# A masked-sum and product kernel: column sums at the tail, and first transfers of 32 and 96 rows in place of 128

## Chip, cores, metric

One Trainium2 chip, one core. The time is that of the device in microseconds (us). Kernels that are compared ran in turn on the same chip, unless it is said otherwise. A run more than 1.5% above the fastest of the same kernel is called slow.

## The reference

```
B, S, D = 8, 8192, 512                    # x: [8, 8192, 512] f32, w: [512, 512] f32
cs  = np.cumsum(x * mask, axis=1)         # mask: position < lengths[b]
mid = cs[b, lengths[b] // 2, :]
out = mid @ w                             # [8, 512]
```

So row b of the output is the sum of the first n = min(lengths // 2 + 1, lengths) rows of x[b], times w. For the lengths drawn here n is 570, 2690, 256, 2057, 905, 3772, 3859 and 571: in whole blocks of 512 rows 1, 5, 0, 4, 1, 7, 7 and 1, and a remainder each.

## The kernel before

A block of 512 rows is loaded as [128 partitions, 4 rows of 512]: 8 KB for each partition, 1 MB in all. TensorE adds it with four matmuls of 8 weight columns in four column groups (eight instructions in the profile, `x8`), so `s_ps` holds four partial sums. SP issues the blocks; ACT issues the remainders. The sequences go in pairs, q = 0 and 1, each side with its own buffers.

```
NP = 6                                              # block buffers for each side
nc.scalar.dma_start(out=wt[:], in_=w.rearrange("(p kc) d -> p kc d", kc=KC)).then_inc(s_w, 16)
nc.sync.dma_start(out=first[:], in_=xf[:BLK].rearrange("(p g) d -> p g d", g=G)).then_inc(s_first, 16)
# (cut) TensorE, for each sequence of each pair
take(pe, s_rem[q], 16 * (len(PARTS) + 1))           # the remainder first
for j in range(G):
    mm = add(j, cur[:, q, B + j * B:2 * B + j * B], rem[:, q, j])
def add_block(k):
    for _ in range(2 if k else 0):                  # fillers, meant to keep the clock up
        pe.matmul(idle_ps[:], lhsT=idle[:, :P], rhs=idle[:], start=True, stop=True)
    take(pe, s_full[q][k], 16)
    for j in range(G):
        mm = add(j, cur[:, q, :B], xt[:, q, k, j])
    mm.then_inc(s_sum, 1)                           # SP waits on it before it refills a buffer
# (cut) tail: DVE copies s_ps to s_sb; four matmuls s_sb^T @ fold; DVE copy; sixteen matmuls with wt; copy; output
```

## Time and profile before

| | before |
|---|---|
| time, first three runs | 88.41, 89.12, 88.33 us |
| profiled run | 89.17 us, span 87.4 us |
| moved | 31.29 MB, mean 358 GB/s over the span |
| second but last block landed | 76.70 us |
| issue of the output | 84.59 us |

The span is what the profile covers; the time is some 1.8 us longer. The lines of the page are in the prediction. From slice 2 to slice 34 the transfers move 356 to 432 GB/s, in most slices 410 or more, so the middle is bound by bytes, and only the start and the tail can change. A transfer has landed when its semaphore has its full count.

### The profile page before, as it was taken

How to read it: one execution, taken by the hardware profiler on the slowest of the kernel's cores; microseconds unless marked ns; L12 is line 12 of the kernel's file. 1: busy time of each engine (PE TensorE's matmuls, PEld its weight loads, DVE VectorE, ACT ScalarE, POOL GpSimd, SP SyncE). 2: the span in 40 equal slices, each digit the busy share in tenths (PEclk: the TensorE clock that was granted, in tenths of full speed). 3: DMA queues.
4: the chain of work that ended last, by engine and by line, in shares of the span. 5: the costliest groups of instructions: out<-in, count | busy, mean ns of one | idle time of the engine just before them, and what ended most of it. 6: DMA issues, size and time to landing. Idle time of an engine off the chain costs nothing. (4 is left out here: it accounts for less than half of the span.)

```text
span 87.4 us, 1387 instructions
## 1 busy us (share of the span) xinstructions
PE 57.3 (66%) x350; PEld 11.0 (13%) x350; DVE 10.6 (12%) x42; ACT 2.0 (2%) x4; POOL 4.4 (5%) x9
## 2 busy tenths in 40 slices
PE   0920355699999798418675569966955556489740
PEld 0220000121111211000210010101110110021520
DVE  3977600000000100000000000000000000000430
ACT  0000000000000000000006000000000000000020
POOL 5940000000000000000000000000000000000000
PEclk9999999999999999999999955599999999965999
DMA  2799999999999999999999999999999999960000
GB/s 30 311 424 356 384 384 408 432 420 424 413 398 416 420 424 428 418 399 417 420 424 428 412 425 424 424 420 420 420 420 424 424 424 420 420 259 0 0 0 11
DMA packets 4694, 31.29 MB, mean 358 GB/s; under 512 B 658, under 2 KB 674, under 8 KB 946
## 3 DMA queue, kind: packets, MB, share of 16 engines
q1 hardware_dynamic: 3762, 27.27, 75.8%
q10 hardware_dynamic: 928, 3.97, 11.7%
q14 instruction: 3, 0.02, 0.1%
q8 instruction: 1, 0.02, 0.1%
HBM read 31.23 MB, written 0.02 MB: 358 GB/s over the span
## 5 line engine op out<-in xcount | busy, mean ns | idle before, releaser
L381 PE MATMUL s_ps<-xt,cur 128*8 128x512 f32 x200 | 31.1, 680 | 12.1 <-PEq L108 12.1
L381 PE MATMUL s_ps<-rem,cur 128*8 128x512 f32 x64 | 11.7, 763 | 6.5 <-PEq L108 6.5
L415 PE MATMUL idle_ps<-idle 128*128 128x512 bf16 x34 | 11.7, 429 | 0.0
L381 PEld LDWEIGHTS s_ps<-xt,cur 128*8 128x8 f32 x200 | 4.3, 90 | 28.2 <-issue 27.9
L355 DVE COPY cur<-table 128x40 f32<-128x40 f32 x8 | 1.4, 184 | 50.4 <-PE s_ps L381 50.4
L381 PE MATMUL s_ps<-first,first_w 128*8 128x512 f32 x8 | 1.9, 1040 | 4.0 <-DVE table L301 4.0
L415 PEld LDWEIGHTS idle_ps<-idle 128*128 128x128 bf16 x34 | 2.0, 100 | 17.8 <-issue 17.8
L381 PEld LDWEIGHTS s_ps<-rem,cur 128*8 128x8 f32 x64 | 1.8, 91 | 15.6 <-issue 15.5
L389 PE MATMUL s_ps<-zero 1*128 1x512 f32 x2 | 2.1, 1132 | 2.3 <-DVE ones L301 2.3
L289 POOL MEMSET rem<- 128x4096 f32 x1 | 3.5, 3512 | 0.0
L301 DVE COPY s_sb<-s_ps 128x256 f32<-128x256 f32 x2 | 0.8, 424 | 19.4 <-PE s_ps L381 19.4
L301 DVE TENSOR_SCALAR n_i<-lens 1x8 int32<-1x8 int32 x1 | 2.8, 2767 | 0.2 <-DMA lens<-in_lengths_dram 0.2
L275 ACT ACT_TABLE_LOAD x1 | 1.3, 1283 | 46.4 <-issue 46.4
L431 PE MATMUL mf_ps<-fold,s_sb 128*128 128x8 f32 x8 | 1.1, 260 | 0.5 <-DVE s_sb L301 0.5
L392 PE MATMUL n_ps<-n_f,ones 1*128 1x8 f32 x2 | 0.6, 368 | 1.2 <-DVE n_f L301 1.2
L278 ACT COPY o_sb<-o_ps 8x128 f32<-8x128 f32 x2 | 0.5, 259 | 36.0 <-PE o_ps L439 36.0
L431 PEld LDWEIGHTS mf_ps<-fold,s_sb 128*128 128x128 f32 x8 | 1.0, 190 | 1.8 <-DVE s_sb L301 1.8
L439 PE MATMUL o_ps<-wt,mf_sb 128*8 128x128 f32 x32 | 1.1, 273 | 0.0
L392 PEld LDWEIGHTS n_ps<-n_f,ones 1*128 1x128 f32 x2 | 0.5, 308 | 2.8 <-DVE n_f L301 2.8
L389 PEld LDWEIGHTS s_ps<-zero 1*128 1x128 f32 x2 | 0.5, 304 | 2.3 <-DVE ones L301 2.3
L439 PEld LDWEIGHTS o_ps<-wt,mf_sb 128*8 128x8 f32 x32 | 0.8, 89 | 0.0
L301 DVE COPY o_sb<-o_ps 8x128 f32<-8x128 f32 x2 | 0.6, 280 | 0.9 <-PE o_ps L439 0.8
(37 smaller groups left out, 6.7 us busy)
## 6 DMA issues: line engine op xcount, KB each, us to landing
xt<-in_x_dram SPq DMA_DIRECT2D x25, 1024.0 KB, 14.3
rem<-in_x_dram ACTq DMA_DIRECT2D x3, 512.0 KB, 7.6
wt<-in_w_dram ACTq DMA_DIRECT2D x1, 1024.0 KB, 6.6
first<-in_x_dram SPq DMA_DIRECT2D x1, 1024.0 KB, 8.4
rem<-in_x_dram ACTq DMA_DIRECT2D x3, 256.0 KB, 6.8
rem<-in_x_dram ACTq DMA_DIRECT2D x3, 128.0 KB, 7.1
rem<-in_x_dram ACTq DMA_DIRECT2D x3, 32.0 KB, 5.7
rem<-in_x_dram ACTq DMA_DIRECT2D x1, 64.0 KB, 6.2
```

What stands on the lines that cost most here:

```text
L275: act.copy(out=warm[:], in_=zero[:, :1])
L278: copy = act.copy(out=o_sb[1][:, j * P:(j + 1) * P], in_=o_ps[64 + 32 * j:64 + 32 * j + B, :P])
L289: pool.memset(rem[:], 0.0).then_inc(s_pool, 1)
L301: do(*args, **kw).then_inc(s_dve, 1)
L355: dve.tensor_copy(out=cur[:, b % 2], in_=table[:, b * WT:(b + 1) * WT]).then_inc(s_cur[b % 2], 1)
L381: return pe.matmul(s_ps[32 * j:32 * j + B], lhsT=weights, rhs=rows, start=False, stop=False, skip_group_check=True, tile_position=(0, 32 * j))
L389: pe.matmul(s_ps[:], lhsT=zero[:, :P], rhs=zero[:], start=True, stop=False, skip_group_check=True)
L392: pe.matmul(n_ps[:, :B], lhsT=ones[:], rhs=n_f[:], start=True, stop=True).then_inc(s_pe, 1)
L415: pe.matmul(idle_ps[:], lhsT=idle[:, :P], rhs=idle[:], start=True, stop=True)
L431: mm = pe.matmul(mf_ps[h][:, i * B:(i + 1) * B], lhsT=s_sb[:, 2 * h + i], rhs=fold[:], start=True, stop=True)
L439: mm = pe.matmul(o_ps[32 * j:32 * j + B, :P], lhsT=mf_sb[:, kc], rhs=wt[:, kc, j * P:(j + 1) * P], start=(kc == 0), stop=(kc == KC - 1), t ...
```

## The change

Intent: (1) bring the first bytes in sooner, with a short first transfer on each queue, 32 rows, two for each of the 16 DMA engines; (2) take the last block out of the sum over rows, so that after it only 16 small matmuls, a transpose and the product follow; (3) keep TensorE's clock up with more fillers (in the profile before, half clock followed stretches in which PE was busy 41% and 43%). Buffers go from six to five a side, and the last block gets a place of its own.

```diff
-    NP = 6
+    NP = 5
-    nc.scalar.dma_start(out=wt[:], in_=w.rearrange("(p kc) d -> p kc d", kc=KC)).then_inc(s_w, 16)
-    nc.sync.dma_start(
-        out=first[:], in_=xf[:BLK].rearrange("(p g) d -> p g d", g=G)
-    ).then_inc(s_first, 16)
+    for at, count in [(0, 32), (32, P - 32)]:
+        part = slice(at, at + count)
+        nc.scalar.dma_start(
+            out=wt[part], in_=w[KC * at:KC * (at + count)].rearrange("(p kc) d -> p kc d", kc=KC)
+        ).then_inc(s_w, 16)
+        nc.sync.dma_start(
+            out=xt[part, 0, 0], in_=xf[G * at:G * (at + count)].rearrange("(p g) d -> p g d", g=G)
+        ).then_inc(s_full[0][0] if at else s_first, 16)
 (cut: SP leaves out the last whole block of the last sequence and loads it at the end, in two halves of
  each partition's rows, to `last`; counts come from a small table; POOL's memset is halved)
+                        keep_busy()                      # two fillers ahead of every remainder
                         take(pe, s_cur[q], 1)
                         take(pe, s_rem[q], 16 * (len(PARTS) + 1))
 (cut)
+                keep_busy()
+                for j in range(4):                       # column sums of all but the last block
+                    if j % 2 == 0:
+                        pe.wait_ge(s_dve, DVE_MASK + 1 + j // 2)
+                    mm = add_column(j, fold[:], s_sb, start=True)
+                with pe.If_cmp(ns[B], 1, "IS_GE"):
+                    keep_busy()
+                    for g in range(G):                   # the last block, 16 matmuls of 128 columns
+                        if g % 2 == 0:
+                            pe.wait_ge(s_last[g // 2], 16)
+                        for j in range(4):
+                            mm = add_column(j, cur[:, 1, :B], last[:, g], start=False)
 (cut: two transposes of 128x64 on DVE in place of the second copy, then the product as before)
```

More of the change, by code (lines that the diff above doesn't have):

```diff
@@ L64 @@
     xt = sb("xt", [P, 2, NP, G, D])
-    first = sb("first", [P, G, D])
+    last = sb("last", [P, G, D])
     rem = sb("rem", [P, 2, G, D])
@@ L68 @@
     lens1 = sb("lens1", [1, 2 * B], I32)
-    warm = sb("warm", [1, 1])
     n_i = sb("n_i", [1, B], I32)
     n_f = sb("n_f", [1, B])
+    cut = sb("cut", [1, 1])
+    blk_i = sb("blk_i", [1, B + 1], I32)
     ones = sb("ones", [1, P])
-    zb = sb("zb", [1, 32], BF16)
     cnt = sb("cnt", [P, B], I32)
@@ L81 @@
     thr = sb("thr", [P, G], I32)
-    first_w = sb("first_w", [P, B])
     idle = sb("idle", [P, D], BF16)
@@ L85 @@
     cur = sb("cur", [P, 2, WT])
-    zero = sb("zero", [1, D])
+    zero = sb("zero", [1, P])
     fold_i = sb("fold_i", [P, B], I32)
     fold = sb("fold", [P, B])
-    s_sb = sb("s_sb", [P, KC, P])
-    mf_sb = sb("mf_sb", [P, KC, B])
+    s_sb = sb("s_sb", [P, D])
+    t_sb = sb("t_sb", [P, KC, 32])
     o_sb = [sb(f"o_sb{h}", [B, D // 2]) for h in range(2)]
     s_ps = ps("s_ps", [P, D])
-    mf_ps = [ps(f"mf_ps{h}", [P, D]) for h in range(2)]
+    t_ps = ps("t_ps", [P, D])
     o_ps = ps("o_ps", [P, D])
@@ L101 @@
     s_cur = [sem(f"cur{q}") for q in range(2)]
-    s_w, s_first, s_len1, s_go, s_out = sem("w"), sem("first"), sem("len1"), sem("go"), sem("out")
+    s_last = [sem(f"last{h}") for h in range(2)]
+    s_zero = [sem(f"zero{q}") for q in range(2)]
+    s_w, s_first = sem("w"), sem("first")
+    s_len1, s_go, s_out = sem("len1"), sem("go"), sem("out")
     s_pool, s_dve, s_pe = sem("pool"), sem("dve"), sem("pe")
@@ L108, in take, with __init__, rows @@
         eng.wait_ge(s, n).then_inc(s, -n)
-    class Counts:
-        def __init__(self, eng, ready, count, loaded=B):
+    class Pairs:
+        def __init__(self, eng, ready, count):
             self.eng = eng
-            self.raw = [eng.alloc_register(f"n_{eng.engine.name}_{i}") for i in range(2 * loaded)]
-            self.regs = self.raw[::2]
+            self.raw = [eng.alloc_register(f"n_{eng.engine.name}_{i}") for i in range(4)]
             self.t = eng.alloc_register(f"t_{eng.engine.name}")
+            self.at = eng.alloc_register(f"pair_{eng.engine.name}")
+            eng.reg_mov(self.at, 0)
             eng.wait_ge(ready, count)
-            eng.load(self.raw, lens1[:, :2 * loaded])
-            self.pair = None
-            if loaded < B:
-                self.pair = eng.alloc_register(f"pair_{eng.engine.name}")
-                eng.reg_mov(self.pair, 0)
-        def without_first(self, base=None):
-            alu, t, n = self.eng.reg_alu, self.t, self.rows(0)
-            alu(t, n, 9, ALU.logical_shift_right)
-            alu(t, t, 1, ALU.min)
-            alu(t, t, 9, ALU.logical_shift_left)
-            alu(n, n, t, ALU.subtract)
-            if base is not None:
-                alu(base, base, t, ALU.add)
-            alu(n, n, 1, ALU.logical_shift_left)
-            alu(n, n, 1, ALU.subtract)
-            alu(n, n, 0, ALU.max)
-        def rows(self, b):
-            n = self.regs[b]
+            eng.load(self.raw, lens1[:, :4])
+        def rows(self, q):
+            n = self.raw[2 * q]
             self.eng.reg_alu(self.t, n, 1, ALU.logical_shift_right)
@@ L147, in rows, with step @@
             return n
-        def next_pair(self):
-            if self.pair is not None:
-                self.eng.reg_alu(self.pair, self.pair, 4, ALU.add)
-                self.eng.reg_alu(self.pair, self.pair, 2 * B - 4, ALU.min)
-                self.eng.load(self.raw, lens1[:, ds(self.eng.snap(self.pair, min_val=0, max_val=2 * B - 4), 4)])
-                return
-            for to, of in zip(self.regs, self.regs[2:]):
-                self.eng.reg_mov(to, of)
+        def step(self):
+            alu, top = self.eng.reg_alu, 2 * B - 4
+            alu(self.at, self.at, 4, ALU.add)
+            alu(self.at, self.at, top, ALU.min)
+            self.eng.load(self.raw, lens1[:, ds(self.eng.snap(self.at, min_val=0, max_val=top), 4)])
     def whole_blocks(eng, n, most, body, k=0):
@@ L163, in whole_blocks @@
                 whole_blocks(eng, n, most, body, k + 1)
-    DVE_SEL, DVE_N, DVE_MASK = 2, 6, 28
+    DVE_SEL, DVE_N, DVE_BLK, DVE_MASK = 1, 5, 10, 31
     DVE_LAST = DVE_MASK + 6
     nc.sync.dma_start(out=lens1[:], in_=lens_words).then_inc(s_len1, 16)
-    nc.scalar.dma_start(out=wt[:], in_=w.rearrange("(p kc) d -> p kc d", kc=KC)).then_inc(s_w, 16)
-    nc.sync.dma_start(
-        out=first[:], in_=xf[:BLK].rearrange("(p g) d -> p g d", g=G)
-    ).then_inc(s_first, 16)
+    for at, count in [(0, 32), (32, P - 32)]:
[6 more added lines that the diff above has]
+        ).then_inc(s_full[0][0] if at else s_first, 16)
     block = nc.Block(no_gpsimd_drain=True)
@@ L183, in _ @@
     def _(sp):
-        ns = Counts(sp, s_len1, 16, loaded=2)
-        sp.sem_inc(s_go, 1)
+        alu = sp.reg_alu
         base, at = sp.alloc_register("sp_base"), sp.alloc_register("sp_at")
         sp.reg_mov(base, 0)
-        ns.without_first(base)
         items = sp.alloc_register("sp_items")
-        sp.reg_mov(items, 2)
+        sp.reg_mov(items, 1)
         until = [[sp.alloc_register(f"until{q}_{k}") for k in range(NP)] for q in range(2)]
@@ L194, in _ @@
             sp.reg_mov(u, 1)
+        has_last, last_at = sp.alloc_register("has_last"), sp.alloc_register("last_at")
+        sp.reg_mov(has_last, 0)
+        sp.reg_mov(last_at, 0)
+        least = sp.alloc_register("sp_least")
+        sp.reg_mov(least, BLK)
+        ns = Pairs(sp, s_len1, 16)
+        sp.sem_inc(s_go, 1)
         with sp.Fori(0, B // 2):
@@ L197, in _, with load @@
                 n = ns.rows(q)
-                sp.reg_alu(items, items, 1, ALU.add)
-                def load_block(k):
-                    sp.wait_ge(s_sum, until[q][k % NP])
-                    sp.reg_alu(items, items, 1, ALU.add)
-                    sp.reg_mov(until[q][k % NP], items)
+                alu(items, items, 1, ALU.add)
+                if q == 0:
+                    alu(n, n, least, ALU.max)
+                    sp.reg_mov(least, 0)
+                else:
+                    with sp.If_cmp(ns.at, 2 * B - 4, "IS_GE"):
+                        alu(has_last, n, 9, ALU.logical_shift_right)
+                        alu(has_last, has_last, 1, ALU.min)
+                        alu(last_at, has_last, 9, ALU.logical_shift_left)
+                        alu(n, n, last_at, ALU.subtract)
+                        alu(last_at, n, ~(BLK - 1), ALU.bitwise_and)
+                        alu(last_at, last_at, base, ALU.add)
+                def load(k):
                     sp.dma_start(
@@ L207, in load_block @@
                     ).then_inc(s_full[q][k % NP], 16)
-                whole_blocks(sp, n, NB, load_block)
-                sp.reg_alu(base, base, S, ALU.add)
-                sp.reg_alu(base, base, ~(S - 1), ALU.bitwise_and)
-            ns.next_pair()
+                def load_block(k):
+                    sp.wait_ge(s_sum, until[q][k % NP])
+                    alu(items, items, 1, ALU.add)
+                    sp.reg_mov(until[q][k % NP], items)
+                    if (q, k) == (0, 0):
+                        with sp.If_cmp(ns.at, 1, "IS_GE"):
+                            load(k)
+                    else:
+                        load(k)
+                whole_blocks(sp, n, NB, load_block)
+                alu(base, base, S, ALU.add)
+            ns.step()
+        with sp.If_cmp(has_last, 1, "IS_GE"):
+            from_rows = rows(sp, at, last_at, 0, BLK).rearrange("(p g) d -> p g d", g=G)
+            for h in range(2):
+                sp.dma_start(
+                    out=last[:, 2 * h:2 * h + 2], in_=from_rows[:, 2 * h:2 * h + 2]
+                ).then_inc(s_last[h], 16)
         sp.wait_ge(s_dve, DVE_LAST)
@@ L219, in _ @@
     def _(act):
-        ns = Counts(act, s_go, 1)
-        t = ns.t
+        alu = act.reg_alu
         base, at = act.alloc_register("act_base"), act.alloc_register("act_at")
         act.reg_mov(base, 0)
-        ns.without_first(base)
         items = act.alloc_register("act_items")
-        act.reg_mov(items, 2)
+        act.reg_mov(items, 1)
         until = [act.alloc_register(f"until_rem{q}") for q in range(2)]
@@ L229, in _ @@
             act.reg_mov(u, 1)
-        act.wait_ge(s_pool, 2)
+        least = act.alloc_register("act_least")
+        act.reg_mov(least, 1)
+        act.memzero(rem[:, 0]).then_inc(s_zero[0], 1)
+        ns = Pairs(act, s_go, 1)
+        t = ns.t
         with act.Fori(0, B // 2):
@@ L233, in _ @@
                 n = ns.rows(q)
+                act.wait_ge(s_zero[q], 1)
                 act.wait_ge(s_sum, until[q])
-                act.reg_alu(items, items, 1, ALU.add)
-                act.reg_alu(until[q], items, 1, ALU.max)
-                act.reg_alu(t, n, 9, ALU.logical_shift_right)
-                act.reg_alu(items, items, t, ALU.add)
+                alu(items, items, 1, ALU.add)
+                alu(until[q], items, 1, ALU.max)
+                alu(t, n, 9, ALU.logical_shift_right)
+                if q == 0:
+                    alu(t, t, least, ALU.max)
+                    act.reg_mov(least, 0)
+                alu(items, items, t, ALU.add)
                 for count, start, step, g in PARTS:
-                    act.reg_alu(t, n, count, ALU.bitwise_and)
+                    alu(t, n, count, ALU.bitwise_and)
                     with act.If_cmp(t, 1, "IS_GE"):
-                        act.reg_alu(t, n, ~(2 * count - 1), ALU.bitwise_and)
+                        alu(t, n, ~(2 * count - 1), ALU.bitwise_and)
                         act.dma_start(
@@ L248, in _ @@
                         act.sem_inc(s_rem[q], 16)
-                act.reg_alu(at, n, ~63, ALU.bitwise_and)
-                act.reg_alu(at, at, base, ALU.add)
-                act.reg_alu(t, n, 63, ALU.bitwise_and)
+                alu(at, n, ~63, ALU.bitwise_and)
+                alu(at, at, base, ALU.add)
+                alu(t, n, 63, ALU.bitwise_and)
                 def load_last(count):
-                    last = rem[3::4, q, 2:] if count > 32 else rem[3:4 * count:4, q, 2:3]
+                    to = rem[3::4, q, 2:] if count > 32 else rem[3:4 * count:4, q, 2:3]
                     act.dma_start(
-                        out=last,
-                        in_=xf[ds(act.snap(at), count)].rearrange("(g p) d -> p g d", g=last.shape[1]),
+                        out=to,
+                        in_=xf[ds(act.snap(at), count)].rearrange("(g p) d -> p g d", g=to.shape[1]),
                     ).then_inc(s_rem[q], 16)
@@ L269, in _ @@
                             act.sem_inc(s_rem[q], 16)
-                act.reg_alu(base, base, S, ALU.add)
-                act.reg_alu(base, base, ~(S - 1), ALU.bitwise_and)
-            ns.next_pair()
-        act.wait_ge(s_dve, DVE_SEL)
-        act.copy(out=warm[:], in_=zero[:, :1])
+                alu(base, base, S, ALU.add)
+            ns.step()
         act.wait_ge(s_pe, B + 5)
@@ L288, in _ @@
         pool.iota(fold_i[:], pattern=[[-1, B]], base=128, channel_multiplier=1).then_inc(s_pool, 1)
-        pool.memset(rem[:], 0.0).then_inc(s_pool, 1)
         pool.memset(idle[:], 1.0).then_inc(s_pool, 1)
+        pool.wait_ge(s_dve, DVE_BLK)
+        pool.memset(rem[:, 1], 0.0).then_inc(s_zero[1], 1)
     @block.vector
@@ L304, in _ @@
         step(dve.memset, zero[:], 0.0)
-        step(dve.memset, zb[:], 0.0)
         assert done == DVE_SEL
@@ L312, in _ @@
         step(dve.tensor_tensor, out=n_f[:], in0=n_i[:], in1=lens1[:, ::2], op=ALU.min)
-        assert done == DVE_N
+        assert done == DVE_N, done
+        step(dve.tensor_copy, out=blk_i[:, :B], in_=n_f[:])
+        step(dve.tensor_scalar, out=blk_i[:, :1], in0=n_f[:, :1], scalar1=BLK, scalar2=None, op0=ALU.max)
+        step(dve.tensor_scalar, out=cut[:], in0=n_f[:, B - 1:], scalar1=BLK, scalar2=None, op0=ALU.is_ge)
+        step(dve.tensor_copy, out=blk_i[:, B:], in_=cut[:])
+        step(dve.scalar_tensor_tensor, out=blk_i[:, B - 1:B], in0=cut[:], scalar=float(-BLK),
+             in1=n_f[:, B - 1:], op0=ALU.mult, op1=ALU.add)
+        assert done == DVE_BLK, done
         step(dve.memset, table[:], 0.0)
@@ L316, in _ @@
         step(dve.memset, tab[:, :, 0:1], 1.0)
-        step(dve.memset, o_ps[:, :P], 0.0)
-        step(dve.memset, first_w[:], 0.0)
+        step(dve.memset, t_ps[:, :P], 0.0)
         step(dve.memset, bits[:], 256)
@@ L342, in _ @@
         step(dve.tensor_copy, out=cnt[:], in_=n_ps[:, :B])
-        step(dve.tensor_scalar, out=first_w[:, :1], in0=cnt[:, :1], scalar1=BLK, scalar2=None,
+        step(dve.tensor_scalar, out=table[:, :1], in0=cnt[:, :1], scalar1=BLK, scalar2=None,
              op0=ALU.is_ge)
@@ L355, in _ @@
             dve.tensor_copy(out=cur[:, b % 2], in_=table[:, b * WT:(b + 1) * WT]).then_inc(s_cur[b % 2], 1)
-        ns = Counts(dve, s_go, 1)
+        n = [dve.alloc_register(f"n_dve_{b}") for b in range(B)]
+        dve.load(n, blk_i[:, :B])
         total, due = dve.alloc_register("total"), dve.alloc_register("due")
-        dve.reg_mov(total, B + 2)
-        ns.without_first()
-        for b in range(B):
-            n = ns.rows(b)
-            dve.reg_alu(n, n, 9, ALU.logical_shift_right)
-            dve.reg_alu(total, total, n, ALU.add)
-        dve.reg_alu(due, total, B + 2, ALU.max)
+        dve.reg_mov(total, B + 1)
+        for r in n:
+            dve.reg_alu(r, r, 9, ALU.logical_shift_right)
+            dve.reg_alu(total, total, r, ALU.add)
+        dve.reg_alu(due, total, B + 1, ALU.max)
         dve.wait_ge(s_sum, due)
-        cols = s_ps[:].rearrange("p (i kc) -> p kc i", kc=KC)
         for h in range(2):
-            step(dve.tensor_copy, out=s_sb[:, 2 * h:2 * h + 2], in_=cols[:, 2 * h:2 * h + 2])
+            step(dve.tensor_copy, out=s_sb[:, 2 * P * h:2 * P * (h + 1)], in_=s_ps[:, 2 * P * h:2 * P * (h + 1)])
+        dve.wait_ge(s_pe, B + 3)
         for h in range(2):
-            dve.wait_ge(s_pe, B + 2 + h)
-            step(dve.tensor_copy, out=mf_sb[:, 2 * h:2 * h + 2].rearrange("p a b -> p (a b)"), in_=mf_ps[h][:, :2 * B])
+            step(dve.transpose, out=t_sb[:, 2 * h:2 * h + 2].rearrange("p k c -> p (k c)"),
+                 in_=t_ps[:, :P].rearrange("p (c k) -> p k c", k=KC)[:, 2 * h:2 * h + 2])
         assert done == DVE_LAST - 2
@@ L383, in add, with keep_busy, add_column @@
                              tile_position=(0, 32 * j))
+        def keep_busy():
+            for _ in range(2):
+                pe.matmul(idle_ps[:], lhsT=idle[:, :P], rhs=idle[:], start=True, stop=True)
+        def add_column(j, weights, row, **kw):
+            return pe.matmul(t_ps[32 * j:32 * j + B, :P], lhsT=weights, rhs=row[:, P * j:P * (j + 1)],
+                             stop=False, skip_group_check=True, tile_position=(0, 32 * j), **kw)
         with pe.Fori(0, 2) as i:
@@ L388, in _ @@
                 pe.wait_ge(s_dve, DVE_SEL)
-                pe.matmul(s_ps[:], lhsT=zero[:, :P], rhs=zero[:], start=True, stop=False,
-                          skip_group_check=True)
+                pe.matmul(s_ps[:], lhsT=zero[:], rhs=zero[:, :1].to_broadcast((1, D)), start=True,
+                          stop=False, skip_group_check=True)
                 pe.wait_ge(s_dve, DVE_N)
                 pe.matmul(n_ps[:, :B], lhsT=ones[:], rhs=n_f[:], start=True, stop=True).then_inc(s_pe, 1)
-                pe.wait_ge(s_pool, 3)
-                ns = Counts(pe, s_go, 1)
-                ns.without_first()
+                pe.wait_ge(s_pool, 2)
+                pe.wait_ge(s_dve, DVE_BLK)
+                ns = [pe.alloc_register(f"n_pe_{b}") for b in range(B + 1)]
+                pe.load(ns, blk_i[:])
                 pe.wait_ge(s_dve, DVE_MASK)
                 pe.wait_ge(s_first, 16)
-                for j in range(G):
-                    mm = add(j, first_w[:], first[:, j])
-                mm.then_inc(s_sum, 1)
                 with pe.Fori(0, B // 2):
                     for q in range(2):
+                        keep_busy()
                         take(pe, s_cur[q], 1)
@@ L409, in _ @@
                         mm.then_inc(s_sum, 1)
-                        n = ns.rows(q)
+                        n = ns[q]
                         def add_block(k):
-                            for _ in range(2 if k else 0):
-                                pe.matmul(idle_ps[:], lhsT=idle[:, :P], rhs=idle[:], start=True,
-                                          stop=True)
+                            if k:
+                                keep_busy()
                             take(pe, s_full[q][k], 16)
@@ L425, in _ @@
                             pe.reg_alu(n, n, 0, ALU.max)
-                    ns.next_pair()
-                for h in range(2):
-                    pe.wait_ge(s_dve, DVE_MASK + 1 + h)
-                    for i in range(2):
-                        mm = pe.matmul(mf_ps[h][:, i * B:(i + 1) * B], lhsT=s_sb[:, 2 * h + i],
-                                       rhs=fold[:], start=True, stop=True)
+                    for to, of in zip(ns[:B], ns[2:B]):
+                        pe.reg_mov(to, of)
+                keep_busy()
[3 more added lines that the diff above has]
+                    mm = add_column(j, fold[:], s_sb, start=True)
+                mm.then_inc(s_pe, 1)
+                with pe.If_cmp(ns[B], 1, "IS_GE"):
+                    keep_busy()
+                    for g in range(G):
[3 more added lines that the diff above has]
+                            mm = add_column(j, cur[:, 1, :B], last[:, g], start=False)
                     mm.then_inc(s_pe, 1)
-                pe.wait_ge(s_w, 16)
+                with pe.Else():
+                    pe.sem_inc(s_pe, 1)
+                pe.wait_ge(s_w, 32)
                 for kc in range(KC):
@@ L438, in _ @@
                     for j in range(4):
-                        mm = pe.matmul(o_ps[32 * j:32 * j + B, :P], lhsT=mf_sb[:, kc],
+                        mm = pe.matmul(o_ps[32 * j:32 * j + B, :P], lhsT=t_sb[:, kc, :B],
                                        rhs=wt[:, kc, j * P:(j + 1) * P],
```

## The prediction

> **What bounds the kernel now.** I read the page first (busy shares, the 40 slices, the chain), then the timeline of the last 13 us, then the arrivals of the DMAs, then quarter-microsecond windows of the start. The slices say that the transfer engines set the middle:
>
> ```profile
> span 87.4 us, 1387 instructions
> PEclk9999999999999999999999955599999999965999
> DMA  2799999999999999999999999999999999960000
> GB/s 30 311 424 356 384 384 408 432 420 424 413 398 416 420 424 428 418 399 417 420 424 428 412 425 424 424 420 420 420 420 424 424 424 420 420 259 0 0 0 11
> ```
>
> One slice is 2.18 us. From slice 2 to 34 DMA is at 90% or more and some 424 GB/s; all 31.29 MB must pass. So the middle cannot shrink: neither kernel changes the rows read. What can change is the ramp at the left and everything after the last byte at the right. The chain of waits agrees, it covers only the tail:
>
> ```profile
> 76.84 4.50 PE s_ps L381 x24
> 81.36 0.44 DVE s_sb L301
> 81.84 1.07 PE mf_ps L431 x8
> 82.91 1.03 PE o_ps L439 x32
> 83.96 0.29 DVE o_sb L301
> ```
>
> The timeline shows what that 4.50 us is:
>
> ```profile
> 76.84 1.52 PE L381 MATMUL s_ps<-xt,cur 128*8 128x512 f32 x8 [1.45 <-PEq L108]
> 78.10 1.97 PE L381 MATMUL s_ps<-rem,cur 128*8 128x512 f32 x8
> 79.80 1.49 PE L381 MATMUL s_ps<-xt,cur 128*8 128x512 f32 x8
> 83.96 0.59 DVE L301 COPY o_sb<-o_ps 8x128 f32<-8x128 f32 x2 [0.84 <-PE o_ps L439]
> 84.59 0.36 SPq L216 DMA_DIRECT2D out_dram<-o_sb  x1
> ```
>
> These are the last block of sequence 6 (the second but last transfer), the remainder of sequence 7 (landed at 51.5), and the only whole block of sequence 7. The trace's arrivals put the last two 1 MB blocks at 76.70 and 79.16. The same group of 8 matmuls takes 1.04 us elsewhere; here it takes 1.5 to 2.0, as the clock is at one half:
>
> ```profile
> 73.86:77.27 3.41, 1.48 (x13) 0.29 (x16) 0.00 (x0) 0.00 (x0) 0.00 (x0) 1.00 1.01 423
> 77.27:80.69 3.42, 3.42 (x22) 0.73 (x16) 0.00 (x0) 0.00 (x0) 0.00 (x0) 0.50 0.14 58
> ```
>
> (Columns: stretch, then busy time of PE, weight load, DVE, ACT, POOL, then granted clock, DMA share, GB/s.) PE was busy only 43% of the stretch before, because the sixth buffer ends the unrolled loop and block 6, its successor, has no filler matmuls ahead of it.
>
> The start, in windows of the same columns:
>
> ```profile
> 1.75:2.00 0.25, 0.00 (x0) 0.00 (x0) 0.17 (x1) 0.00 (x0) 0.25 (x1) 1.00 1.23 197
> 2.00:2.25 0.25, 0.00 (x0) 0.00 (x0) 0.12 (x1) 0.00 (x0) 0.25 (x1) 1.00 0.61 98
> 2.25:2.50 0.25, 0.18 (x1) 0.19 (x2) 0.25 (x1) 0.00 (x0) 0.25 (x1) 1.00 0.17 33
> 2.50:2.75 0.25, 0.25 (x1) 0.25 (x2) 0.25 (x1) 0.00 (x0) 0.25 (x1) 1.00 0.67 197
> 2.75:3.00 0.25, 0.25 (x1) 0.05 (x1) 0.25 (x1) 0.00 (x0) 0.25 (x1) 1.00 0.51 164
> 3.00:3.25 0.25, 0.25 (x1) 0.00 (x0) 0.25 (x1) 0.00 (x0) 0.25 (x1) 1.00 1.03 393
> ```
>
> The first data packet starts at 1.93 but the full rate only at about 3.0. The packet records show why: eight engines start at 1.93 to 2.01, six of them need over 1 us for their first 8 KB instead of 0.31, and the other eight start only at 2.69 to 2.81.
>
> [...] the half-speed stretches are 3.41 and 6.83 us long, and lie on one grid; stretches of 41% and 43% busy were followed by half speed, one of 1.65 in 3.42 us (48%) was not. [...]
>
> **The change, part by part.**
>
> *Ramp.* Missing bytes up to 3.0: full rate from 1.93 would be 1.07 us x 424 = 454 KB; the five windows moved (197+98+33+197+164) x 0.25 = 172 KB; 282 KB / 424 = 0.66 us lost. If descriptors come in row order, the first 64 rows took 2.69 - 1.93 = 0.76 us, 12 ns a row, so 32 rows spread over all engines need an estimated 0.38 us. I expect 0.45 us back, and a little from SP issuing its first block load about 1 us earlier (its 13 register moves now come before the wait for the lengths), which may soften the dip to 295 GB/s near 8 us: 0.5 us in all. All later arrivals move forward by it: the last block of sequence 6 from 76.70 to 76.2.
>
> *Buffers.* Five instead of six per side, but the first block and the last one have places of their own use. SP's longest wait for a buffer is 12.2 us with transfers queued all the while; at 44.5, where the fifth buffer matters, four blocks are still on their way. No starvation: 0.
>
> *Setup.* DVE's first integer instruction (2.77 us beside the 3.51 us POOL memset) gets short, five small ones of some 0.19 are added. The mask is done near 8.5 instead of 10.2, but PE then waits for the first remainder, landed at 13.9. Off the path: 0.
>
> *Tail.* The last block leaves the sum over rows: after it only 16 matmuls of 128 columns, two transposes and the product follow. But sequence 6 keeps its seventh block, and after that PE has in program order: filler, remainder 7, column sums of s_sb, filler, the last block. Counted from the arrival of block 6 (T), at full clock:
>
> - start 0.14 (76.84 - 76.70); 8 matmuls, issue to issue 0.98; two fillers 0.54; remainder 1.04: 2.70.
> - DVE copies s_ps in two parts, 0.03 + 0.44 + 0.44: 3.61; a filler pair lies beside it. Column sums of the first half run meanwhile; the second half 0.04 + about 0.25: 3.9.
> - branch about 0.1, filler pair 0.5: 4.5. The last block landed at T + 2.5, so no wait.
> - 16 matmuls of 128 columns = 32 instructions, like the product's 32 (1.06): 5.5.
> - first transpose 0.25 to 0.3 (DVE copies: 0.17 for 16 columns, 0.42 for 256), second beside the first half of the product; product 1.0: 6.85.
> - copy out 0.02 + 0.59, 0.03 to the issue: 7.5.
>
> Before, in this profile, it is 84.59 - 76.70 = 7.89. But this is a profile with a half clock in its tail, and its run took 89.17. At full clock the old tail is bound by the last arrival (T + 2.46): 0.14 + 1.04 + 0.03 + 0.44 + 0.04 + 1.07 + 1.03 + 0.02 + 0.62 = 4.43, so T + 6.89. That is 1.0 shorter, and fits the two timed runs of 88.33 and 88.41 beside 89.12. So against a fast run the new tail costs 7.5 - 6.9 = +0.6, against a half-clock one -0.4. With -0.5 of the ramp: +0.1 or -0.9. The new kernel has fillers ahead of all remainders and block 6 too; only block 5 has none, so its poorest 3.41 us stretch holds 1.04 + 0.6 = 48% and I expect full clock in most runs. Span: 76.2 + 7.5 + 2.78 (the old issue of the output to the end) = 86.5; add the 1.80 between the profiled run's span and its time: 88.3. I take 88.2.
>
> **The rivals.**
>
> *The last arrival sets the end (the intent).* If the PE work between were hidden, the end would be the last arrival plus 16 matmuls, transpose, product and copy: 78.7 + 0.14 + 1.0 + 0.3 + 1.0 + 0.65 = 81.8, 2.8 us before the old issue: about 86.4, faster by over 2%. For it: the last block's path is truly short. Against it: the listed PE and DVE work after block 6 adds up to 4.5 us, while the block comes after 2.5. It takes a PE chain 2 us shorter than every row here shows.
>
> *The clock goes to half in the new tail.* With 48% against 43% that failed, the margin is small, and the grid's place differs by run. Half clock over one window costs some 1.7 us of PE work: 89.9; over two, 91.
>
> *The ramp gains nothing,* as first bytes wait on something other than descriptors, or the 96-row transfers then stall the engines: 88.7.
>
> **Range and chances.** Three terms are uncertain: ramp 0 to 0.8, tail sum +-0.5, clock. That gives 87.2 to 89.4. Over 2% faster needs 86.64 or less, only the first rival does that: 0.1. Over 2% slower needs 90.2, the clock in most runs: 0.07. Within 2%: 0.83.
>
> **What would show it.** Ramp: windows from 1.9 to 3.0 near full rate, and the last block of sequence 6 landing about 0.5 earlier. Tail: after that landing, remainder 7, two DVE copies, column sums, filler and the last block follow with no wait on the DMA of the last block; output issue 7.5 after it, and the last matmuls begin about 2 us after their data landed. Wrong if the last block's matmuls wait for DMA, if PEclk falls in the last four slices, or if DMA shows gaps near 21 or 45 us (starvation by five buffers).

The sum, 76.2 + 7.5 + 2.78 + 1.80 = 88.3, taken as 88.2, comes from the traces and from estimates on them. But the 0.45 us of the ramp rested on an assumption, that transfers of 32 and 96 rows keep all 16 engines at the full rate; no run had shown it.

## More of the kernel before

One more view is needed for what follows, the windows of two microseconds in the first part. The columns are: stretch and length, busy time (and count) of PE, weight load, DVE, ACT, POOL, then granted clock, DMA share and GB/s. Before:

```profile
3.00:5.00 2.00, 1.38 (x2) 0.00 (x0) 1.97 (x2) 0.00 (x0) 2.00 (x2) 1.00 1.01 422
5.00:7.00 2.00, 0.59 (x2) 0.50 (x2) 1.35 (x9) 0.00 (x0) 0.36 (x1) 1.00 1.02 422
7.00:9.00 2.00, 0.00 (x0) 0.00 (x0) 1.66 (x11) 0.00 (x0) 0.00 (x0) 1.00 0.99 332
9.00:11.00 2.00, 0.77 (x4) 0.12 (x8) 1.21 (x8) 0.00 (x0) 0.00 (x0) 1.00 0.99 393
```

The last two numbers matter: the engines are busy all the time (share about 1), and move 332 to 422 GB/s.

## The result, and the profile after

The changed kernel takes 92.50 us (median of 4, 92.11 to 92.64) against 88.55 us (median of 4, 88.33 to 89.12). The ratio is 1.043, 95% interval 1.037 to 1.049: slower. A ratio is the mean time of one kernel's fast runs over that of the other's in the same rounds, so not quite the ratio of the medians quoted. The prediction of 88.2 us, with 7% for slower, was wrong.

The page of the changed kernel; one slice is 2.26 us here:

```profile
span 90.3 us, 1478 instructions
PEclk9999999999999999996699999999999999999996
DMA  3999999999999999999999999999999999970000
GB/s 58 218 243 236 265 361 415 422 414 435 414 413 418 425 421 425 414 414 408 423 428 421 414 421 417 421 425 425 414 421 435 421 421 417 408 296 4 0 0 11
```

The DMA line looks the same as before: 90% and more from slice 1 on. The line below it doesn't: slices 1 to 4 have 218 to 265 GB/s where the kernel before has 311 to 424. The engines are busy, but each packet takes longer. From slice 6 on the rate is that of before. The windows (columns as above), after:

```profile
3.00:5.00 2.00, 1.61 (x4) 0.65 (x2) 1.31 (x11) 1.99 (x2) 1.40 (x1) 1.00 1.00 209
5.00:7.00 2.00, 0.00 (x0) 0.00 (x0) 1.66 (x11) 0.29 (x1) 0.41 (x1) 1.00 1.03 262
7.00:9.00 2.00, 0.85 (x2) 0.14 (x2) 1.08 (x7) 0.00 (x0) 0.00 (x0) 1.00 1.00 254
9.00:11.00 2.00, 0.16 (x1) 0.00 (x0) 0.00 (x0) 0.00 (x0) 0.00 (x0) 1.00 1.05 262
```

Up to 13 us (the window 11 to 13 has 342 GB/s after and 376 before) these add to 2 x (209+262+254+262+342) = 2658 KB against 2 x (422+422+332+393+376) = 3890 KB: 1232 KB less, which is 2.9 us at 424 GB/s. That is nearly the whole loss: the second but last block lands at 79.67 instead of 76.70 us, 2.97 later, and the span is 2.9 us longer. In the packet records of this stretch the 8 KB packets take 590 to 650 ns (those of the 32-row transfer of x, means of half-microseconds) and mostly 470 to 580 ns (those of the 96-row transfers), against 309 ns for most packets of the kernel before.

The tail is the predicted chain, here from the chain of waits (start, duration, what):

```profile
79.81 1.04 PE s_ps L409 x8
80.86 0.54 PE idle_ps L416 x2
81.39 1.04 PE s_ps L409 x8
82.46 0.43 DVE s_sb L325
...
83.40 0.39 PE t_ps L420 x4
83.79 0.54 PE idle_ps L416 x2
84.33 1.03 PE t_ps L420 x32
```

The last block landed at 82.15 and was taken at 84.26 (its first weight load), so it waited 2.1 us for PE. The output is issued at 87.53, 7.86 us after the landing of the second but last block, against 7.89 in the profile before: the new tail gave nothing and cost nothing beside a half-clock tail.

### The profile page after: what moved, and what is told of

It is laid out like the page before. It is cut to its first block, busy times and chain, and to the rows that moved or that the text cites. A ratio compares the mean times of both kernels' runs of the same rounds, so it can differ in the third digit from the quotient of the medians.

```text
span 90.3 us, 1478 instructions
## 1 busy us (share of the span) xinstructions
PE 57.1 (63%) x394; PEld 11.1 (12%) x394; DVE 8.2 (9%) x45; ACT 3.7 (4%) x5; POOL 2.8 (3%) x9
## 5 line engine op out<-in xcount | busy, mean ns | idle before, releaser
L409 PE MATMUL s_ps<-xt,cur 128*8 128x512 f32 x200 | 27.6, 626 | 16.2 <-PEq L114 16.2
L416 PE MATMUL idle_ps<-idle 128*128 128x512 bf16 x54 | 17.4, 405 | 4.6 <-DVE table L325 3.5
L409 PE MATMUL s_ps<-rem,cur 128*8 128x512 f32 x64 | 10.5, 736 | 6.0 <-PEq L114 6.0
L416 PEld LDWEIGHTS idle_ps<-idle 128*128 128x128 bf16 x54 | 3.1, 98 | 28.0 <-issue 28.0
L409 PEld LDWEIGHTS s_ps<-rem,cur 128*8 128x8 f32 x64 | 1.0, 88 | 10.5 <-issue 10.5
L250 ACT ACTIVATE rem<-rem 128x2048 uint32<-128x2048 uint32 x1 | 1.9, 1910 | 0.0
L314 POOL MEMSET rem<- 128x2048 f32 x1 | 1.8, 1804 | 1.7 <-DVE blk_i L325 1.7
L485 PE MATMUL o_ps<-wt,t_sb 128*8 128x128 f32 x32 | 1.1, 273 | 0.5 <-DVE t_sb L325 0.5
L420 PE MATMUL t_ps<-last,cur 128*8 128x128 f32 x32 | 1.1, 273 | 0.0
L485 PEld LDWEIGHTS o_ps<-wt,t_sb 128*8 128x8 f32 x32 | 0.8, 89 | 0.7 <-issue 0.7
```

The costliest lines, as they stand in the source:

```text
L250: act.memzero(rem[:, 0]).then_inc(s_zero[0], 1)
L314: pool.memset(rem[:, 1], 0.0).then_inc(s_zero[1], 1)
L409: return pe.matmul(s_ps[32 * j:32 * j + B], lhsT=weights, rhs=rows, start=False, stop=False, skip_group_check=True, tile_position=(0, 32 * j))
L420: return pe.matmul(t_ps[32 * j:32 * j + B, :P], lhsT=weights, rhs=row[:, P * j:P * (j + 1)], stop=False, skip_group_check=True, tile_posit ...
L485: mm = pe.matmul(o_ps[32 * j:32 * j + B, :P], lhsT=t_sb[:, kc, :B], rhs=wt[:, kc, j * P:(j + 1) * P], start=(kc == 0), stop=(kc == KC - 1) ...
```

## The theory and its rivals

Theory, *partitions*: the slow packets come from which partitions a transfer fills. The windows of the changed kernel have 209 to 262 GB/s, 0.49 to 0.62 of 424, and its packets of 32 rows of x take about twice the time (590 to 650 ns). My guess, which no run had shown when e3 was set up: transfers that fill only one half of the partitions, 0 to 63 or 64 to 127, share half of the rate; a set that is spread evenly over both has all of it. (The expectations on record gave this theory a name and a mechanism that no run shows; both are cut there, and the figures that come first, without a name, are this theory's.) An estimate from the guess and the measured rate: packets of the 32 rows take 2 x 309 = 618 ns; of the 96 rows 64 lie in one half. At half of 424 GB/s: 2 x 64 rows x 8 KB / 212 = 4.9 us and 2 x 32 x 8 KB / 212 = 2.5 us, together 7.4 instead of 4.95 us for these 2.1 MB, so some 2.5 us lost.

Rivals: *size*, few rows for each engine or two queues that alternate on the engines slow every packet, wherever it goes; and *tail or buffers*, the slowness comes with the rest of the change.

## The experiments

Twelve kernels, all with correct results. Times are medians of all runs, slow ones too; "before" is of the same rounds. One run of four was slow in e10 and in e11, one of six in e12, two of four in e9, and of the kernel before four of seven in the rounds of e10 and e11, three of eleven in those of e12, one of seven elsewhere. The ratios leave slow runs out, but judge them among the timed rounds alone, so that of e9 counts three runs (89.83, 90.84, 91.01) of which two are slow beside its profiled run of 88.87. Its fast runs, 88.87 and 89.83, lie 0.6% above the mean of the fast ones of before, 88.78.

| run | this, us | before, us | ratio (95%) |
|---|---|---|---|
| e1 changed, first transfers whole | 89.25 | 88.58 | 1.008 (1.001 to 1.015) |
| e2 before, first transfers split | 91.43 | 88.58 | 1.030 (1.020 to 1.040) |
| e3 changed, 4 x 32 rows, every fourth partition | 91.33 | 88.58 | 1.032 (1.025 to 1.039) |
| e4 e1, all blocks in partition halves | 148.5 (one look) | 89.14 | |
| e5 e1, all blocks in even and odd partitions | 90.82 (one look) | 89.14 | |
| e6 e1, first transfers in partition halves | 93.76 | 89.07 | 1.058 (1.048 to 1.067) |
| e7 e1, first transfers in even and odd partitions | 90.91 | 89.07 | 1.023 (1.014 to 1.033) |
| e8 e1, no filler ahead of the last block | 88.94 | 89.07 | 1.000 (0.991 to 1.010) |
| e9 e8, last remainder earlier | 90.33 | 89.07 | 1.020 (1.009 to 1.032) |
| e10 e9 with six buffers | 91.66 | 89.38 | 1.030 (1.011 to 1.049) |
| e11 e9, blocks ahead of remainders, three pairs | 93.45 | 89.38 | 1.053 (1.034 to 1.073) |
| e12 e9, blocks ahead of remainders, first pair | 91.22 | 89.20 | 1.028 (1.022 to 1.035) |

### e1 and e2: which part of the change costs the time

e1 puts the whole first transfers back into the changed kernel; e2 puts the split into the kernel before.

```diff
 # e1, on the changed kernel
-    for at, count in [(0, 32), (32, P - 32)]: ...
+    nc.scalar.dma_start(out=wt[:], ...).then_inc(s_w, 16)
+    nc.sync.dma_start(out=xt[:, 0, 0], in_=xf[:BLK]...).then_inc(s_full[0][0], 16)
 # e2, on the kernel before: the same loop over (0, 32), (32, 96) as in the change, to wt and first
```

> The changed kernel with its first transfers whole again (128 rows each, one for the weights, one for the first block); tail, fillers, five buffers as changed. If the split alone cost the time, packets of 8 KB take 309 ns again from 3 us on, block 6 of sequence 6 lands at about 76.7 (79.67 in the changed kernel), and the time is about 89.1 us (the changed tail's 7.86 us from that landing to the issue of the output against 7.89 in the half-clock tail and some 6.9 in a full-clock tail of before). If the tail, the fillers or the five buffers cost it, it stays at about 92 us.

> The kernel before with only its two first transfers split into 32 and 96 rows. If the split alone costs the time: 8 KB packets of 500 to 640 ns between 3 and 11 us, the last blocks land some 3.0 us later, about 91.5 us. If it needs the new tail: 88.5 us.

Measured: e1 89.25 us, with the second but last block at 76.68 us and the output issued 7.85 us later (84.53). e2 91.43 us; the windows from 3 to 11 us have 213, 258, 246 and 270 GB/s. The same window of e2, then of e1:

```profile
5.00:7.00 2.00, 0.59 (x2) 0.49 (x2) 1.35 (x9) 0.00 (x0) 0.36 (x1) 1.00 1.03 258
5.00:7.00 2.00, 0.00 (x0) 0.00 (x0) 1.65 (x11) 0.00 (x0) 0.44 (x1) 1.00 1.00 418
```

Each came out, to 0.2 us, as expected if the split alone costs the time. It costs 2.85 us with the old tail (91.43 - 88.58) and 3.25 with the new (92.5 - 89.25, two chips); tail, fillers and buffers together cost 0.8%. The rival *tail or buffers* is out as the cause of the 4%.

The intent of the split was met, though: in the quarter-microsecond windows from 1.75 to 3.00 us e2 moved (230+295+393+393+262) x 0.25 = 393 KB against 172 KB before, 0.5 us of full rate; the changed kernel 254 KB, 0.2 us; e1, with whole transfers, 180 KB. The gain is there, uneven, and far smaller than what the slow packets take back.

### e3: as short a first transfer, to every fourth partition

```diff
-    for at, count in [(0, 32), (32, P - 32)]: ...
+    for i in range(4):
+        nc.scalar.dma_start(out=wt[i::4], in_=w.rearrange("(p kc) d -> p kc d", kc=KC)[i::4]).then_inc(s_w, 16)
+        nc.sync.dma_start(
+            out=xt[i::4, 0, 0], in_=xf[P * i:P * (i + 1)].rearrange("(p g) d -> p g d", g=G)
+        ).then_inc(s_full[0][0] if i == 3 else s_first, 16)
```

The first block is whole (n of sequence 0 is 570), so all its rows have weight 1 and may lie in any partition.

> The changed kernel with the first transfers cut into four of 32 rows each, two rows for each DMA engine, but to every fourth partition (0, 4, 8 ... then 1, 5, 9 ...), the block's rows in memory read in the same order. [...] packets take 310 to 400 ns and the time is 88.5 to 89.3 us, though these transfers are more and smaller. Rival, size: few rows for each engine, or two queues with work on the same engines at once, slow the packets: packets of 500 ns and more, 91.5 us or more.

Measured: most packets as the theory has it. Their median is 309 ns in every half-microsecond from 3 to 8 us; the mean is 309 to 320 in five of these ten stretches and 351 to 555 in the other five (4.0 to 6.5 us), and near 490 from 8 to 9 us, as single packets take up to 1.45 us. The windows from 3 to 11 us have 348, 320, 340 and 418 GB/s against 209 to 262. The time failed: 91.33 us, where the theory said 88.5 to 89.3 and size 91.5 or more. Its page shows another hole: slices 10 and 12 have 283 and 272 GB/s, 22 to 29 us into the span. So e3 speaks for the theory by its packets only, and it brought up a second matter, to which e9 to e12 belong.

### e4 and e5: the same split in every block, to two sets of partitions

Both load each block in two transfers of 256 rows (64 partitions each), from the same source ranges in the same order. Only the destination differs.

```diff
+                    for h in range(2):
                         sp.dma_start(
-                            out=xt[:, q, k % NP],
-                            in_=rows(sp, at, base, k * BLK, BLK).rearrange("(p g) d -> p g d", g=G),
+                            out=xt[64 * h:64 * h + 64, q, k % NP],      # e4
+                            out=xt[h::2, q, k % NP],                    # e5
+                            in_=rows(sp, at, base, k * BLK + 256 * h, 256).rearrange("(p g) d -> p g d", g=G),
```

> The kernel e1 with every block of 512 rows loaded in two transfers of 64 partitions each, first 0 to 63, then 64 to 127. [...] packets take about 618 ns and the blocks land every 3.7 to 4.9 us instead of 2.48, so clearly over 110 us. Size as the rival has it: the same time as e5, whatever that is.

> The same as e4 with the same source ranges in the same order, but the halves go to the even and then to the odd partitions[...] packets stay near 310 ns, the time near that of e1, 89 to 90 us. Size as the rival has it: the same time as e4.

The rates by slice, of e4 (a slice is 3.67 us):

```profile
GB/s 125 319 226 222 225 239 217 241 246 219 230 214 230 219 230 244 215 239 226 230 223 232 232 223 219 232 228 214 230 223 226 217 232 223 221 226 228 139 0 7
```

and of e5 (2.23 us):

```profile
GB/s 29 328 412 401 277 393 414 429 427 420 424 404 420 427 416 420 415 413 412 423 420 423 407 429 423 420 423 420 423 423 420 420 423 411 394 64 0 0 0 11
```

148.5 against 90.8 us; over the whole stream about half the rate in e4, and full rate in e5 for as many and as small transfers. In e4 slice 1, at 319, still holds the whole transfer of the weights; slices 2 to 36 lie between 214 and 246. In the steady part the median 8 KB packet of SP's queue takes 587 ns in e4 and 312 in e5, and in e4 512 KB land every 2.35 us or so (41.56, 43.91, 46.27), 1 MB in 4.7, as expected. TensorE's clock is lower in e4 (0.60 granted from 50 to 100 us), but the DMA engines are never short of work there (share 1.02), so that is not what bounds it. This is the clearest run: size, count, order and source are the same, and which partitions a transfer fills makes a factor of 1.85 in the rate (420 GB/s from 20 to 70 us against 228 from 50 to 100). (e5 is one look; it lies about 1.5 us above e1, and its slice 4 has a dip to 277 GB/s, which I did not follow.)

### e6 and e7: the same pair at the start only

```diff
+    for h in range(2):
+        part = slice(64 * h, 64 * h + 64)      # e6
+        part = slice(h, P, 2)                  # e7
+        nc.scalar.dma_start(out=wt[part], in_=w.rearrange("(p kc) d -> p kc d", kc=KC)[part]).then_inc(s_w, 16)
+        nc.sync.dma_start(out=xt[part, 0, 0], in_=xf[256 * h:256 * h + 256]...)
```

> The kernel e1 with each of its two first transfers (weights, first block) cut into partitions 0 to 63 and then 64 to 127. [...] 8 KB packets take about 618 ns from 3 us to about 12 us, 2.1 MB need some 10 us instead of 5, and the time is about 93 to 94 us. Rival (few rows for each engine, two queues at once): the same time as e7.

> The same number, size and order of transfers as e6, with the same source ranges for the first block, but to the even and then the odd partitions. [...] packets near 309 ns from 3 us on, the time that of e1 or up to 1 us more (89.3 to 90.3 us), as two more issues delay what SP and ACT issue next. Rival: as slow as e6.

Windows of e6, then of e7 (columns as above):

```profile
5.00:7.00 2.00, 0.00 (x0) 0.00 (x0) 1.66 (x11) 0.60 (x1) 0.41 (x1) 1.00 0.96 197
7.00:9.00 2.00, 0.00 (x0) 0.00 (x0) 1.09 (x7) 0.00 (x0) 0.00 (x0) 1.00 1.02 221
9.00:11.00 2.00, 0.86 (x2) 0.14 (x2) 0.00 (x0) 0.00 (x0) 0.00 (x0) 1.00 1.01 205
```

```profile
5.00:7.00 2.00, 0.00 (x0) 0.00 (x0) 1.66 (x11) 0.60 (x1) 0.41 (x1) 1.00 0.98 389
7.00:9.00 2.00, 0.62 (x2) 0.13 (x2) 1.08 (x7) 0.00 (x0) 0.00 (x0) 1.00 1.12 328
9.00:11.00 2.00, 0.39 (x1) 0.00 (x0) 0.00 (x0) 0.00 (x0) 0.00 (x0) 1.00 0.89 369
```

e6 takes 93.76 and e7 90.91 us on the same chip, in the same rounds: 2.85 us for the choice of partitions (in e7 the weights' source rows alternate with the partitions, too; those of x do not). e6's packets take 600 to 655 ns from 3.5 to 12 us (538 near 7 us), so it came out as expected. e7 took 0.6 us more than the top of what I expected (two issues on a queue took 0.81 and 0.88 us in the changed kernel, one 0.37 and 0.41 before); its packets are near 310 ns in most half-microseconds, but for 375 at 5 us and 480 and 916 from 7.5 to 8.5 us, and it has the same hole as e3 (slices 10 to 12: 334, 329 and 274 GB/s). With e4 and e5 this shows that the partitions slow the packets: the rival *size* does not explain a difference between two kernels of the same transfers. It is not out for the rest of the time. Against before, e6 is at 1.058, e7 at 1.023 and the whole transfers of e1 at 1.008, so some 3.5 of the 5 points that e6 costs come from the partitions, and some 1.5 from splitting at all. From 3 to 13 us e1 moved 4148 KB, e7 3746 and e3 3698, about 1 us of full rate less; I did not find out why. What makes the partitions matter, no run shows.

### e8: is the new tail a chain of work?

```diff
                 with pe.If_cmp(ns[B], 1, "IS_GE"):
-                    keep_busy()
```

> The kernel e1 without the two filler matmuls ahead of the last block's 16 matmuls. If the tail is a chain of PE and DVE work after block 6, as predicted, and not a wait for the last transfer, 0.54 us go: about 88.7 us. If the last transfer sets the end: unchanged, 89.25 us.

Measured: 88.94 us, a ratio of 1.000 to before (e1: 1.008, on another chip). The trace shows the step: from the landing of the second but last block (77.76) to the issue of the output (84.94) 7.18 us instead of 7.85 in e1, 0.67 less for a filler pair of 0.54. The time fell by less than its own scatter, and in the profiled run that block landed 1.1 us later than in e1. So the chain is shown, the saving in time is not.

### e9 to e12: a shorter tail, and what it ran into

e9 takes the remainder of sequence 7 ahead of the blocks of sequence 6, so that nothing but the last block's own path is left after block 6.

```diff
-                with pe.Fori(0, B // 2):
-                    (for each q: remainder q, blocks q)
+                with pe.Fori(0, B // 2 - 1):
+                    (for each q: remainder q, blocks q)
+                (last pair: remainder 0, remainder 1, blocks 0, blocks 1)
```

> The kernel e8 with the remainder of sequence 7 moved ahead of the blocks of sequence 6 on PE (last pair only; SP's counts adjusted). Then after block 6 only its matmuls, two copies, the column sums and the last block remain: landing + 1.2 + 0.9 + 0.4 = 2.5, which meets the last arrival at + 2.5; then half the last block 0.6, transposes 0.4, product 1.1, copy 0.65: issue of the output 5.3 us after the landing of block 6 instead of 7.86, about 86.7 us, faster than both kernels. If the tail's length is set otherwise, 88.7 us as e8.

Measured: 90.33 us, two of the four runs slow (the two fast ones 88.87 and 89.83); no profile shows what the slow ones did. In the profiled run, a fast one, the tail did shrink, to 6.07 us (landing 78.02, issue 84.09; 5.3 was expected, and the chain has 0.87 us of issue ahead of the fillers), but the landing came 1.3 us later than in e1, and most of the gain was gone. Windows of e9 (columns as above):

```profile
22.00:24.00 2.00, 2.00 (x18) 0.23 (x10) 0.00 (x0) 0.00 (x0) 0.00 (x0) 1.00 0.94 324
24.00:26.00 2.00, 1.84 (x15) 0.34 (x12) 0.00 (x0) 0.00 (x0) 0.00 (x0) 1.00 0.96 310
```

The queue runs low there: SP could issue the first block of sequence 3 only at 21.53 us, once PE was through with the first block of sequence 1, whose buffer it takes. The share stays at 0.94 and 0.96, since single packets take up to 1.8 us (from 22 to 28 us; the median stays at 309 to 312 ns): again a busy share hides the loss. PE is late since it waits for the first remainder (landed at 15.34) and then works at about half its pace, 1.89 and 1.71 us for its first two groups of eight matmuls against 1.04 later. The page shows a clock of 9 tenths there, but the trace has no clock record before 18.5 us. e10 asks whether five buffers are the reason (`NP = 6`), e11 whether PE's late start is (blocks ahead of remainders in the first three pairs, with SP's and ACT's counts adjusted).

> The kernel e9 with six buffers for each side instead of five. e9 lost 1.5 us of transfer time between 22 and 30 us (slices of 347, 293 and 359 GB/s) as the queue ran dry. If five buffers are the reason, the dip goes and the time falls by 1.3 us or more, below 89 us. If the reason is that PE is late with the first block of sequence 1, whose buffer the first block of sequence 3 takes with six as with five, the dip stays and the time is that of e9.

> The kernel e9 with the blocks of a sequence ahead of its remainder on PE in the first three pairs (counts of SP and ACT adjusted). The first blocks have landed by 9.3 and 12.6 us, the first remainders only at 15.3, so PE frees the first block's buffer of sequence 1 earlier: SP's issue for sequence 3 at about 18.5 instead of 21.5 us, no dip between 22 and 30 us, block 6 of sequence 6 landed at 76.7 to 77.0 instead of 78.0, and with the same 6.1 us of tail about 87.5 us, faster than both kernels. If the dip has another cause, 90 us as e9.

e10: 91.66 us, the dip still there (slices 10 to 12: 249, 372 and 315 GB/s), so the number of buffers is not it. e11, windows:

```profile
22.00:24.00 2.00, 1.46 (x11) 0.26 (x10) 0.00 (x0) 0.00 (x0) 0.00 (x0) 1.00 1.02 426
24.00:26.00 2.00, 0.29 (x2) 0.00 (x0) 0.00 (x0) 0.00 (x0) 0.00 (x0) 1.00 1.00 418
```

SP's issue came at 18.92 and the dip is gone, as expected. But the time is 93.45 us: now the remainder of sequence 7, whose buffer came free later, landed only at 70.4 us, PE waited for it ahead of the blocks of sequence 6, and the transfers stood nearly still (slices 31 to 33: 90, 0 and 195 GB/s). e12 reorders the first pair alone.

> The kernel e9 with the blocks ahead of the remainders in the first pair of sequences only; e11 did so in three pairs, lost its dip between 22 and 30 us, but then waited for the remainder of sequence 7 (landed at 70.4) and ran dry from 70 to 77 us. Here both should be gone: SP's issue for sequence 3 at about 19 us, full rate from 20 to 76 us, block 6 of sequence 6 landed at 76.7 to 77.0, the tail 6.1 us as in e9, the time about 87.5 us, 1 to 2% under the kernel before and 5% under the changed one. If the transfers run dry at another place, 89 us or more.

91.22 us: no dip between 22 and 30 us, but a hole further on, again behind a remainder that came late (issued at 29.47, landed at 34.96; slices 16 to 18: 333, 60 and 359 GB/s). The expectation failed. In e11 and in e12 the order moved the hole to where another buffer came free late. None of these kernels beats the kernel before; e8 equals it, and so do the fast runs of e9 within their scatter.

## Why the prediction was wrong, point by point

- *What bounds the kernel*: right. The middle is bound by bytes; the loss came in at the ramp and went undiminished to the end (2.97 us at the second but last landing, 2.9 us in the span).
- *Ramp*: this step failed. It counted engines and took 424 GB/s for granted whatever partitions a transfer fills (the assumption above), and it expected 0.45 us back, and 0.5 in all. The engines were busy (share 1.00 to 1.05 from 3 to 11 us), the rate was 209 to 262 GB/s. The gain before 3.0 us was 0.2 us (0.5 in e2); the packets after it took 1.5 to 2.1 times as long, and cost 2.9 us. Partitions 0 to 31, and two thirds of 32 to 127, lie in one half of the 128; the pair e4/e5 shows the dependence on partitions with all else equal, and e6/e7 shows it at the start.
- *The rate*: the 424 GB/s was read off transfers that fill all 128 partitions; that partition halves have it too was assumed. Halves cost a factor of 1.85 in the steady state (e4), and 2.85 us at the start (e6 against e7).
- *The third rival* had the right place ("the 96-row transfers then stall the engines") and 0.5 us for it, where 2.9 was measured. It got no chance of its own.
- *Buffers, no starvation*: true of the changed kernel (slices 9 to 13 have 413 to 435 GB/s), but partly since its transfers were late anyway. Kernels with a faster start (e3, e7) or another order (e9) ran low near 22 to 30 us. The margin was smaller than I said (at 44.5 us five blocks were on their way, not four); it is PE's late start, not the number of buffers (e10, e11), that sets it.
- *Tail*: mechanism right, and no wait on the last transfer, as predicted against the first rival. The sum was 7.5 us, measured 7.86: the column sums ended at +4.12 where I had 3.9; 0.14 of issue lay between the first transpose and the product; the product took 1.10 instead of 1.0. Full clock in the tail: right (the last slices of PEclk up to the output are 9).
- *Half clock in the new tail*: did not happen in the profiled run, nor in e1. The place of the grid does differ: the half-speed stretches begin at 49.97 and 77.27 us before, at 41.11 and 88.90 after; from 41.11 to 77.27 it is 10.6 times 3.41 us, so it is not one grid.

The sum of the prediction, corrected by what was measured: 88.2 + (0.5 - 0.2) for the ramp + 2.9 for the packets + 0.4 for the tail = 91.8, against 92.11 in the profiled run, from which these terms are read, and 92.5 as the median; the rest is no larger than the scatter of before (88.33 to 89.12).

## What to carry to other kernels

For a DMA, count not only rows and engines but which partitions it fills: contiguous halves ran here at about half the rate (e4, 228 GB/s), every second partition at the full one (e5, 420 GB/s), with the engines busy in both, so read the GB/s beside the share. If a transfer must be cut, cut it along each partition's bytes (not tried at the start here; the last block's two halves were cut so, and landed at 80.94 and 82.15 us, 0.5 MB in 1.21 us, 433 GB/s, which is full rate) or take every second or fourth partition. At the start no cut that was tried beat the whole transfers of e1. A fix of the start also shifts everything later: look for buffers that come free too late before counting on a gain.

## What the traces show besides

- TensorE's clock, by PE's busy time in each 3.41 us window from the first clock record on. Before: full-speed windows of 41% and 43% (46.55 to 49.97 and 73.86 to 77.27 us) were followed by half speed, as was the last one, after the last matmul (84.10 to 87.51, 0%); all others, 48% and more, by full speed; of the half-speed windows one of 79% was followed by half speed, two of 100% by full speed. After: 39% and 31% by half speed, all from 46% up by full speed; the one half-speed window, of 100%, by full speed. My count in the traces of all fourteen kernels: full-speed windows of up to 43% were followed by half speed (26 of them; one of 43% in e4 was not), all from 46% up by full speed; half-speed windows of up to 79% were followed by half speed, all from 82% up by full speed.
- A transpose of 128x64 f32 out of PSUM on DVE took 0.25 us (mean of two, changed kernel).
